# Equal row blocks, interleaved inner tiles and later transposes in the expert stage of a two-layer diffusion transformer

## The chip, the cores and the metric

One core of one Trainium2 chip runs the whole program. The metric is the device time of one execution in microseconds (us), from the first instruction to the end of the program. TensorE (PE) multiplies, ScalarE (ACT) and VectorE (DVE) do the elementwise work, GpSimd (POOL) issues the indirect transfers, SyncE (SP) issues the weight loads.

## The reference, cut to what matters

The model has two layers over 512 image tokens and 256 context tokens, width 1024. Both layers end in a feed-forward part; in the second it is a mixture of 8 experts, of which each token uses 2:

```
gates = sum over the top 2 experts of one_hot * softmax(top logits)
out   = sum over e of gates[:, e] * (silu(x @ w1[e]) * (x @ w3[e])) @ w2[e]
h     = h + g2 * out
```

An expert's inner width is 1408, that is 11 inner tiles of 128. Its first product (w1 and w3) makes the 11 inner tiles, its second product (w2) takes them back to 1024 columns, that is 8 output tiles of 128.

## The kernel before, in words

The kernel computes each expert only for the tokens that chose it. The expert stage runs from about 1290 us to the end. `CAPS` (L33) gives the slots of the eight steps of the stage, in the order in which they run: 176, 192, 96, 176, 112, 152, 136, 128. A step's slots are cut into row blocks of at most 128 (`moe`, L1972): 128 and 48 for 176 slots, 128 and 64 for 192, 24 and 8 remain in the second block of 152 and 136; 96, 112 and 128 are one block.

For each step the rows of its tokens are gathered by an indirect DMA per block (`gather`, L1793), transposed on TensorE and scaled on ScalarE (`prep`, L1821 and L1825, tiles `xtp`, `xaf`, `xT`) while the step before is at its seventh inner tile (`mid`). `expert` (L1832) then works with the tokens in the free dimension:

- First product: for each of 11 inner tiles j, 48 matmuls (8 depth tiles, two matrices, three passes of the split fp16 weights, `mm1` L336) into a PSUM tile `mps` with three buffers (tag "m"). `evac` follows one tile later: ScalarE's silu into `ms` (L1847), VectorE's product into `mgf` (L1848), and after inner tiles 3, 7 and 10 a cast to `mgT` on ScalarE (L1853) and its remainder on VectorE (L1854). The second product reads `mgT`.
- Second product: for each of 8 output tiles d, 33 matmuls (11 inner tiles k, three passes) into `mps2`, of the same tag. `evac2` (L1873) follows one tile later: ScalarE copies PSUM into `my` with the gate (L1876), TensorE transposes `my` block by block into `ytp` (L1880, PSUM tag "t", two buffers), VectorE copies it with the token's weight into `yr` (L1884).
- After the last output tile (`add_rows`, L2009) one indirect accumulating DMA per block adds `yr` to the output in DRAM (L2019). The last step does it in two parts, columns 0 to 639 after d = 4 and the rest after d = 7. Each of these waits for the landing of the one before, as they all write the output.

Weights come as fp32 through `Stream`: SP loads a block (L246), ScalarE casts it to fp16 (`whi`, `whix` or `aT`, L269) and VectorE makes the remainder (`wlo`, `wlox` or `aT`, L274). A load starts when a staging buffer is free again; five blocks are split ahead of the one in use in this stage.

The order in which an engine meets its instructions isn't simply that of the text. The framework plans it: it goes through the instructions with the order of the text as priority, takes for an engine the first one that is ready by its modelled durations, and writes the result out as a fixed order with semaphore waits. A tile whose buffer is still in use waits in this plan until the readers of the older tile are placed. On the chip the engine then keeps this order.

## Time and profile before

| | us |
|---|---|
| median of three runs | 1780.31 |
| lowest and highest | 1778.89 and 1789.47 |
| the profiled execution's own time | 1788.69 |
| its span, first to last instruction | 1786.8 |

The profile is of the one execution in the third line, which lies at the upper end of the runs; all times below are microseconds from the start of its span. PEld are TensorE's weight loads, which overlap its matmuls. The granted clock is the share of 2.4 GHz at which TensorE was let run. A wait names the waiting instruction and the one that released it, in the form out<-in. "L342" is the line of the helper that issues most matmuls, so these are told apart by their tiles: `mps<-xT` is the first product, `mps<-mgT` the second.

### The profile page before, as it was taken

The numbers are of one execution on the slowest core, as the hardware profiler recorded it, in microseconds if no ns is written. First come the engines' busy times: TensorE is split into PE (matmuls) and PEld (weight loads), VectorE is DVE, ScalarE is ACT, GpSimd is POOL, SyncE is SP. The second block draws the span as 40 slices with busy tenths as digits, with TensorE's granted clock in tenths as the row PEclk, the third lists the DMA queues.
The fourth block names the chain that finished last, engine by engine and source line by source line (L and its number), as shares of the span: only waits on it lengthen the run. The fifth ranks groups of instructions, "written<-read, shape, count | busy, mean of one in ns | idle before, by whom it ended". The sixth has DMA issues, their size and how long they took to land. (4 is left out here: it accounts for less than half of the span.)

```text
span 1786.8 us, 36195 instructions
## 1 busy us (share of the span) xinstructions
PE 1668.7 (93%) x15124; PEld 1170.3 (65%) x15124; DVE 1251.0 (70%) x2463; ACT 883.1 (49%) x1420; POOL 156.1 (9%) x102
## 2 busy tenths in 40 slices
PE   3999999999999999999999999989789999999997
PEld 1444666555566665555555466447579988989997
DVE  6784899877665444333147999696898588788884
ACT  6564555262222222111254667564666577677773
POOL 1100000000000000000000000451210113101201
PEclk9999999999999999999999999999799999999999
DMA  8413342534333442233312201101569788899893
GB/s 322 160 51 100 104 166 95 212 117 143 142 129 131 142 142 96 73 112 112 115 61 79 95 1 48 70 3 54 189 204 337 240 312 334 303 330 336 313 337 109
DMA packets 51801, 286.82 MB, mean 161 GB/s; under 512 B 5824, under 2 KB 10944, under 8 KB 27568
## 3 DMA queue, kind: packets, MB, share of 16 engines
q1 hardware_dynamic: 47328, 271.74, 41.8%
q0 software_dynamic: 3296, 10.95, 2.7%
q8 instruction: 120, 1.97, 0.4%
q10 hardware_dynamic: 1008, 1.77, 0.3%
q14 instruction: 49, 0.40, 0.1%
HBM read 272.57 MB, written 11.08 MB: 159 GB/s over the span
## 5 line engine op out<-in xcount | busy, mean ns | idle before, releaser
L342 PEld LDWEIGHTS <-whi 128*128 128x128 f16 x5184 | 469.7, 99 | 185.3 <-issue 10.8
L342 PE MATMUL f<-yT,whi 128*128 128x512 f16 (+1 forms) x1408 | 325.5, 326 | 1.5 <-ACT af L438 1.5
L342 PEld LDWEIGHTS <-wlo 128*128 128x128 f16 x2592 | 255.6, 99 | 90.4 <-issue 2.2
L274 DVE SCALAR_TENSOR_TENSOR wlo<-wst,whi 128x512 f16<-128x512 f32 (+2 forms) x154 | 236.8, 1549 | 68.1 <-ACT whi L269 67.6
L269 ACT ACTIVATE whi<-wst 128x2048 f16<-128x2048 f32 (+2 forms) x152 | 199.4, 1331 | 111.1 <-PE f L342 72.8
L342 PE MATMUL f<-yT,wlo 128*128 128x512 f16 (+1 forms) x704 | 229.1, 326 | 0.0
L375 DVE SCALAR_TENSOR_TENSOR adjk<-wst,srow 128x1024 bf16<-128x1024 f32 x96 | 117.3, 1221 | 98.4 <-DMA wst<-in_w_adr_dram 97.2
L342 PE MATMUL f<-gT,whi 128*128 128x512 f16 (+1 forms) x704 | 164.4, 326 | 0.0
L342 PE MATMUL mps<-xT,whi 128*128 128x176 f16 (+6 forms) x1472 | 149.0, 229 | 3.8 <-DVE mgf L1848 3.7
L342 PE MATMUL mps<-xT,wlo 128*128 128x176 f16 (+6 forms) x736 | 143.0, 229 | 0.0
L342 PE MATMUL f<-gT,wlo 128*128 128x512 f16 (+1 forms) x352 | 114.7, 326 | 0.0
L342 PEld LDWEIGHTS <-aT 128*128 128x128 f16 x1584 | 106.8, 99 | 5.3 <-issue 4.5
L467 DVE TENSOR_TENSOR h<-h,ytp 128x256 f32<-128x256 f32 (+1 forms) x48 | 24.3, 507 | 109.2 <-PE ytp L465 108.9
L2019 POOL DMA_INDIRECT out_dram<-yr,sidx x14 | 54.4, 3885 | 358.3 <-DVE yr L1884 215.3
L342 PE MATMUL cvps<-aT,whi 128*128 128x512 f16 (+1 forms) x384 | 82.6, 328 | 2.8 <-ACT Kl L632 2.3
L342 PEld LDWEIGHTS <-whix 128*128 128x128 f16 x992 | 81.4, 98 | 2.9 <-issue 2.5
L1082 ACT CAST gT<-g 128x512 f16<-128x512 f32 (+1 forms) x23 | 14.0, 608 | 131.0 <-DVE g L1079 131.0
L274 DVE SCALAR_TENSOR_TENSOR wlo<-wstx,whi 128x2048 f16<-128x2048 f32 (+2 forms) x42 | 68.7, 1651 | 14.0 <-ACT whi L269 11.4
L342 PE MATMUL mps<-xT,aT 128*128 128x176 f16 (+6 forms) x1056 | 74.4, 231 | 2.3 <-DVE mgf L1848 2.3
L342 PE MATMUL mps<-mgT,whi 128*128 128x176 f16 (+6 forms) x704 | 73.0, 227 | 0.9 <-ACT mgT L1853 0.9
L342 PE MATMUL mps<-mgT,wlo 128*128 128x176 f16 (+6 forms) x352 | 68.1, 227 | 0.0
L269 ACT ACTIVATE whi<-wstx 128x2048 f16<-128x2048 f32 (+2 forms) x42 | 57.7, 1401 | 17.6 <-PE mps L342 16.3
(398 smaller groups left out, 3490.1 us busy)
## 6 DMA issues: line engine op xcount, KB each, us to landing
wst<-in_w_m_dram SPq DMA_DIRECT2D x38, 1024.0 KB, 6.2
wstx<-in_w_m_dram SPq DMA_DIRECT2D x33, 1024.0 KB, 6.2
wst<-in_w_adr_dram SPq DMA_DIRECT2D x32, 1024.0 KB, 4.9
wst<-in_w_f_dram SPq DMA_DIRECT2D x22, 1024.0 KB, 4.8
wst<-in_w_m_dram SPq DMA_DIRECT2D x27, 704.0 KB, 6.0
wstx<-in_w_m_dram SPq DMA_DIRECT2D x25, 704.0 KB, 6.1
aT<-in_w_m_dram SPq DMA_DIRECT2D x17, 1024.0 KB, 6.2
wst<-in_w_ada_dram SPq DMA_DIRECT2D x12, 1024.0 KB, 4.9
```

Of the source, the lines that this page charges most:

```text
L269: nc.scalar.activation(h, x, AF.Copy, scale=self.scale)
L274: nc.vector.scalar_tensor_tensor(out=l, in0=x, scalar=SW, in1=h, op0=OP.mult, op1=OP.subtract)
L342: mm(ps[:, s0:s0 + sn], w[:, k, :], a[:, kk, s0:s0 + sn], start=first and p == 0, stop=last and p == 2)
L375: nc.vector.scalar_tensor_tensor(out=jk, in0=st[:, j * D:(j + 1) * D], scalar=1.0, in1=self.srow[:, t, :], op0=OP.mult, op1=OP.mult, accum ...
L467: nc.vector.tensor_tensor(out=hs, in0=hs, in1=tp[:, 0:w].rearrange("p (t c) -> p t c", t=nt), op=OP.add)
L1082: nc.any.tensor_copy(gh, g[:, 0:sn])
L2019: self.nc.gpsimd.indirect_dma_start(out=to, out_offset=bass.IndirectOffsetOnAxis(ap=self.sidx[0:sn, e, s:s + 1], axis=0), in_=yr[0:sn, s, ...
```

## The change

It has three parts, all in the expert stage.

- `moe` cuts a step of more than 128 slots into two equal blocks: 88 and 88, 96 and 96, 76 and 76, 68 and 68. Steps of 128 or fewer keep one block. In `route`, the rows to which unused slots are sent are now counted from the same base in both blocks, so that L1765 reads the first column of the table for both.
- In `expert` the second product's matmuls are issued by a new function `part` over a list of inner tiles. For the first two output tiles the text now gives inner tiles 0 to 7 of d = 0, then 0 to 7 of d = 1, then 8 to 10 of d = 0 and 8 to 10 of d = 1. From d = 2 on, the 33 matmuls of a tile follow one another as before.
- `evac2` only makes `my`; the transposes, the copies into `yr` and the call that starts the scatter move to `rows`, which stands at the head of a later iteration. The transposes of a tile d stood behind the matmuls of tile d + 1; they now stand behind those of d + 2. For d = 5, 6 and 7 they all stand behind the matmuls of d = 7. `my` keeps two buffers (`nb` is 2 here).

```diff
--- before.py
+++ after.py
@@ -1762,7 +1762,7 @@
                 x = rp.tile([128, 1], F32, name="free", tag="free", bufs=2)[0:sn]
                 V.tensor_scalar(x, ip[0:sn, s, i, 1:2], -1.0, 1.0, op0=OP.mult, op1=OP.add)
                 y = rp.tile([128, 1], F32, name="to", tag="to", bufs=2)[0:sn]
-                V.tensor_scalar(y, cst[0:sn, tko + i:tko + i + 1], float(NL), None, op0=OP.add)
+                V.tensor_scalar(y, cst[0:sn, tko:tko + 1], float(NL), None, op0=OP.add)
                 V.scalar_tensor_tensor(out=y, in0=y, scalar=x, in1=ip[0:sn, s, i, 0:1], op0=OP.mult, op1=OP.add)
                 if s == NE - 1:
                     V.tensor_scalar(y, y, 8.0, None, op0=OP.mult)
@@ -1872,8 +1872,12 @@
 
         def evac2():
             d, ps = py.pop(0)
-            y = mp.tile([128, cm], F32, name="my", tag="my", bufs=2)[:, 0:C]
+            y = mp.tile([128, cm], F32, name="my", tag="my", bufs=nb)[:, 0:C]
             nc.scalar.activation(y, ps[:, 0, 0:C], AF.Copy, scale=gate[:, d, 0:1])
+            ys.append((d, y))
+
+        def rows():
+            d, y = ys.pop(0)
             tp = pp.tile([128, max(2, len(slots)), 128], F32, name="ytp", tag="t", bufs=2)
             dd = slice(d * 128, (d + 1) * 128)
             for s, (s0, sn) in enumerate(slots):
@@ -1884,15 +1888,35 @@
                     nc.vector.tensor_scalar(yr[0:sn, s, dd], tp[0:sn, s, :], wt[0:sn, s:s + 1], None, op0=OP.mult)
             done(d, yr)
 
+        def part(w, ps, ks):
+            for k in ks:
+                self.mm1(ps[:, 0], *w, k, gT[:, 0], gT[:, 1], seg, k == 0, k == 10)
+
+        ys = []
+        w0 = []
         for d in range(8):
-            wh, wl = (z.rearrange("p (k c) -> p k c", k=11) for z in w2(d))
+            if d > 1 and len(ys) > nb - 1:
+                rows()
+            w = [z.rearrange("p (k c) -> p k c", k=11) for z in w2(d)]
             ps = pp.tile([128, 2, CB], F32, name="mps2", tag="m", bufs=3)
-            for k in range(11):
-                self.mm1(ps[:, 0], wh, wl, k, gT[:, 0], gT[:, 1], seg, k == 0, k == 10)
+            if d < 2 and nb > 1:
+
+                part(w, ps, range(8))
+                w0.append((w, ps))
+                if d == 0:
+                    continue
+                for i in range(2):
+                    part(*w0[i], range(8, 11))
+                    py.append((i, w0[i][1]))
+                evac2()
+                continue
+            part(w, ps, range(11))
             if py:
                 evac2()
             py.append((d, ps))
         evac2()
+        while ys:
+            rows()
 
     def overflow(self):
 
@@ -1969,7 +1993,8 @@
 
     def moe(self, ctx):
         nc, tc = self.nc, self.tc
-        self.slots = [[(0, min(C, 128))] + ([(128, C - 128)] if C > 128 else []) for C in CAPS]
+
+        self.slots = [[(0, C // 2), (C // 2, C // 2)] if C > 128 else [(0, C)] for C in CAPS]
         self.eid = {}
         res = self.A['out'][0:NL].rearrange("(t p) c -> t p c", p=128)
         for t in range(4):
```

## Rows read from the trace of the kernel before

**Rows 1.** The head of the page: the span, then TensorE's busy time, its share of the span and its instructions.

```profile
span 1786.8 us, 36195 instructions
...
PE 1668.7 (93%) x15124; PEld 1170.3 (65%) x15124; DVE 1251.0 (70%) x2463; ACT 883.1 (49%) x1420; POOL 156.1 (9%) x102
```

**Rows 2.** Busy time by stretch, in the expert stage, two answers one under the other: the stretch, its length, then busy us and (x instructions) of PE, PEld, DVE, ACT, POOL, and at the end the granted TensorE clock (1.00 is 2.4 GHz, 0.50 is 1.2 GHz), the DMA share and GB/s.

```profile
1350.00:1450.00 100.00, 98.18 (x1167) 93.83 (x1165) 71.65 (x76) 61.58 (x71) 6.62 (x3) 1.00 0.81 290
1500.00:1750.00 250.00, 241.98 (x3653) 231.05 (x3651) 212.83 (x223) 182.78 (x219) 42.70 (x11) 1.00 0.92 328
...
1470.00:1475.00 5.00, 5.00 (x34) 3.42 (x34) 2.35 (x4) 2.51 (x6) 0.00 (x0) 0.50 1.04 359
1475.00:1480.00 5.00, 5.00 (x64) 4.91 (x65) 3.06 (x4) 3.10 (x6) 2.49 (x2) 0.51 0.72 254
1480.00:1485.00 5.00, 5.00 (x121) 5.00 (x118) 3.42 (x4) 3.94 (x5) 0.00 (x0) 1.00 0.70 224
```

**Rows 3.** Who TensorE waited for between 1330 us and the end: waiting line, releaser, us in total, how often, the longest.

```profile
PE mps L342 <- DVE mgf L1848: 6.6, 7, 3.7
PE ytp L1880 <- ACT my L1876: 5.4, 12, 1.1
PE mps L342 <- ACT mgT L1853: 1.9, 5, 0.5
PE ytp L1880 <- DVE yr L1884: 1.9, 8, 0.4
```

**Rows 4.** Who the queue of weight loads (SP) waited for between 1340 us and the end, the longest of the list; L246 is the line that issues a weight load.

```profile
SPq L246 <- DVE yr L1884: 142.2, 48, 6.5
SPq L246 <- DVE mgf L1848: 129.2, 51, 5.1
```

**Rows 5.** TensorE in order of time at the start of the second product of the first expert (176 slots): start, length, the merged instructions, their number, and in brackets the idle time before and its releaser.

```profile
1355.24 3.73 PE L342 MATMUL mps<-mgT,aT 128*128 128x176 f16 x47
1359.38 0.39 PE L342 MATMUL mps<-mgT,aT 128*128 128x176 f16 x3 [0.41 <-ACT mgT L1853]
...
1363.11 0.33 PE L1880 MATMUL ytp<-ident,my 128*128 128x128 f32 x1 [0.25 <-ACT my L1876]
...
1364.04 0.27 PE L1880 MATMUL ytp<-ident,my 128*128 128x128 f32 x1
```

**Rows 6.** The same for the fourth expert (176 slots).

```profile
1542.28 1.98 PE L342 MATMUL mps<-mgT,aT 128*128 128x176 f16 x24
1544.10 0.32 PE L342 MATMUL mps<-mgT,whi 128*128 128x176 f16 x2
...
1544.56 0.32 PE L342 MATMUL mps<-mgT,whi 128*128 128x176 f16 x2
1545.28 0.24 PE L342 MATMUL mps<-mgT,aT 128*128 128x176 f16 x1 [0.41 <-ACT mgT L1853]
```

**Rows 7.** ScalarE, then VectorE, over the same moment as group 5, in order of time.

```profile
1355.37 1.38 ACT L269 ACTIVATE whix<-wstx 128x1408 f16<-128x1408 f32 x1 [2.06 <-PE mps L342]
...
1358.69 0.64 ACT L1853 ACTIVATE mgT<-mgf 128x528 f16<-128x528 f32 x1 [1.74 <-DVE mgf L1848]
...
1356.78 1.63 DVE L274 SCALAR_TENSOR_TENSOR wlox<-wstx,whix 128x1408 f16<-128x1408 f32 x1 [1.76 <-ACT whix L269]
```

**Rows 8.** The third expert (96 slots), in order of time: TensorE's longest wait for a transpose, then ScalarE.

```profile
1491.01 0.32 PE L1880 MATMUL ytp<-ident,my 128*96 128x128 f32 x1 [1.12 <-ACT my L1876]
...
1488.81 1.91 ACT L269 ACTIVATE whix<-wstx 128x2048 f16<-128x2048 f32 x1 [1.04 <-PE mps L342]
1490.63 0.56 ACT L1876 ACTIVATE my<-mps,gate 128x96 f32<-128x96 f32 x2
...
1492.88 0.57 ACT L1876 ACTIVATE my<-mps,gate 128x96 f32<-128x96 f32 x2
```

**Rows 9.** Groups by form: the transposes of TensorE, of the gathered rows (xtp, weights of the block's rows, the block's columns streamed) and of the second product (ytp, weights of the block's columns, 128 streamed): line, engine, operation, forms, count, busy us and mean ns of one, idle us before and its releasers.

```profile
L1880 PE MATMUL ytp<-ident,my 128*128 128x128 f32 x48 | 14.1, 294 | 3.4 <-ACT my L1876 1.8 <-DVE yr L1884 0.9
...
L1821 PE MATMUL xtp<-ident,xg 128*128 128x128 f32 x40 | 12.6, 320 | 2.2 <-ACT xaf L1825 1.8
...
L1880 PE MATMUL ytp<-ident,my 128*48 128x128 f32 x16 | 4.5, 286 | 0.5 <-DVE yr L1884 0.3
...
L1821 PE MATMUL xtp<-ident,xg 48*128 48x48 f32 x8 | 2.6, 319 | 0.0
...
L1821 PE MATMUL xtp<-ident,xg 96*128 96x96 f32 x8 | 2.1, 280 | 0.2
...
L1821 PE MATMUL xtp<-ident,xg 8*128 8x8 f32 x8 | 1.8, 223 | 0.0
```

**Rows 10.** The end, in order of time: TensorE, VectorE and GpSimd at the last expert's transposes and its two scatters; the last row is of the chain that ended last, the landing of the first scatter.

```profile
1770.93 0.28 PE L1880 MATMUL ytp<-ident,my 128*128 128x128 f32 x1
...
1772.89 0.28 PE L1880 MATMUL ytp<-ident,my 128*128 128x128 f32 x1
...
1775.89 0.35 DVE L1884 TENSOR_SCALAR yr<-ytp,ws 128x128 f32<-128x128 f32 x1 [0.38 <-PE ytp L1880]
...
1771.88 1.59 POOL L2019 DMA_INDIRECT out_dram<-yr,sidx  x1 [27.11 <-DVE yr L1884]
1778.05 1.56 POOL L2019 DMA_INDIRECT out_dram<-yr,sidx  x1 [4.58 <-DMA out_dram<-yr,sidx]
...
1771.88 5.41 DMA out_dram<-yr,sidx
```

## The prediction

> **What bounds the kernel now.** I read the head of the page first, then busy time by stretch, then TensorE's waits, then the waits of the load queue, and last the moments at which the change acts. TensorE is busy 93% of the span [rows 1], and in the expert stage more: 98.18 of 100 us in the first two experts and 241.98 of 250 us from 1500 to 1750, at a granted clock of 1.00 [rows 2]. VectorE and ScalarE stand at 212.83 and 182.78 of the same 250 us, so both have room; DMA stands at 0.92. Is it the loads that bound the stage? The load queue says no: its longest waits, 142.2 and 129.2 us, are for VectorE, behind whose instructions a staging buffer comes free [rows 4]. Loads start when TensorE and the engines that split weights make room, and in the list of TensorE's waits no weight appears [rows 3]. So the stage goes at TensorE's pace, and time saved on TensorE's queue is saved at the end, as long as the splits follow.
>
> What is there to save? From 1330 us on TensorE waits 5.4 us for `my` before transposes (12 times), 1.9 us for `yr`, 1.9 us for the cast `mgT`, and 6.6 us for `mgf`, of which one wait alone is 3.7 us [rows 3]; that one is in a first product, which the change doesn't touch. What the change aims at is then 5.4 + 1.9 + (6.6 − 3.7) = 10.2 us, 0.6% of the span, and it can't remove more than that by itself.
>
> **The change, part by part.**
>
> Interleaved inner tiles. The text now asks for 24 matmuls of d = 0, 24 of d = 1, and then inner tiles 8 to 10, which need the last cast. But the order on TensorE is planned, and the trace shows that the plan already does this: in the first expert 47 recorded matmuls of the second product run before the first one that waits for `mgT`, not 24 [rows 5]. The text of before would give 24 (8 inner tiles by 3 passes). So for this expert nothing changes, and the wait of 0.41 us stays: it comes from ScalarE's 1.38 us split and VectorE's 1.63 us split, which run while the last silu and product are due, so that the cast starts only at 1358.69 [rows 7]. No more cover is to be had either, as `mps` has three buffers and the last inner tile still holds one. In the fourth expert the plan put fewer in front: 24, then 8 of the next tile, up to 1544.9, and then 0.41 us of waiting [rows 6]. Sixteen more matmuls at (1544.10 − 1542.28) / 24 = 0.076 us are 1.2 us, more than that wait: it goes. The waits of this kind sum to at most 1.9 + 2.9 = 4.8 us [rows 3] over eight experts; if three experts are like the fourth, with 0.35 us each, about 1 us goes. Bounds: 0 (the plan draws the same order again) and 4.8 us. I take 1, nearer to the first expert's row, since the cover is the same 48 there.
>
> Transposes one tile later. 104 transposes stay 104; their copies and scatters stay too, only their place moves. The trace shows them already some way into the next tile's matmuls (1363.11 and 1364.04 with ten between, and the first still waited 0.25 us for `my`) [rows 5]. One tile later `my` has another 33 matmuls of time, 2.5 us at the pace of 0.076 us worked out above. The waits for `my` were at most 1.1 us each [rows 3], so nearly all of the 5.4 us should go. Not where ScalarE itself is behind: in the third expert it makes two `my` in 0.56 us, then splits for 1.91 us, then makes two again, at 1490.63 and 1492.88 [rows 8], 2.25 us apart, so that there ScalarE's splits set the pace; the longest wait, 1.12 us, moves rather than goes. I leave 1.1 us standing and take 5.4 − 1.1 = 4.3 us. Bounds: 5.4, and 0 if the later place only meets the next instruction that is late. What is queued behind such a transpose? All of TensorE's matmuls. What does `my` wait for? With two buffers, ScalarE's copy of tile d + 2 now waits for the transposes of d; those stand at the very point where the matmuls of d + 2 are done, so ScalarE loses about the length of two transposes, and the splits behind it are covered by its idle 67 of 250 us [rows 2]. The waits for `yr` (1.9 us) come from the second transpose of a tile and its two PSUM buffers; these stay, and I count 0 for them.
>
> Equal blocks. `ytp` takes as long for 48 columns as for 128 (286 and 294 ns), so two blocks cost two transposes, before and after: 0. `xtp` does depend on its columns: 128 and 48 cost 320 + 319 ns, and two of 88 by the row for 96 cost 2 x 280 = 560; 128 and 8 cost 320 + 223 = 543, and two of 68 by the same row 560 [rows 9]. Over eight depth tiles that is −0.6 us for one step and +0.1 us for another. With four steps affected the sum is between −2 and +1 us; these durations overlap with neighbours and partly lie in a slow-clock stretch, so I take 0. VectorE, ScalarE and GpSimd issue as many instructions as before; the gathers and scatters keep their number, and only the rows in each are shared out evenly. They are hidden, except for the last expert's, and that one has 128 slots, one block, and stays as it is.
>
> The end. Here the change costs. The last step's first scatter starts after d = 4. Its transpose is at 1770.93, the next one at 1772.89: one tile is 1.96 us. The second scatter has its rows ready at 1775.89 + 0.35 = 1776.24, but it starts at 1778.05, since it waits for the first one's landing, 5.41 us after 1771.88 [rows 10]. So the end hangs on the transpose of d = 4, which moves one tile back: +1.96 us, and the slack is nil. Bounds: +1.96, and +0.2 if the plan pulls that transpose forward to where it stood. The matmuls of d = 6 have priority in the text and are ready all the time, so I take +2.0. The three transposes that now follow the last matmul (d = 5, 6, 7, 0.3 us each) end before that scatter lands and cost nothing.
>
> The clock. At 1470 to 1480, after transposes with a wait among them, the granted clock is 0.50 and 0.51, the 1.2 GHz level, and TensorE runs 64 matmuls in 5 us where the next 5 us hold 121 at 1.00 [rows 2]. Through the transposes of the second products, which have matmuls between them, it stays at 1.00 (1350 to 1450) [rows 2]. The Trainium skill (TensorE: Matmul & The Clock Gate, Part 4: PE-mode transpose) says that a transpose doesn't count as work for the clock as a matmul does. By that rule, six transposes drawn together behind d = 7 could lose the clock; the rows agree for the stretch at 1470 and give no case of it in a second product. In the sum I put 0 for it, as the plan has the next expert's matmuls to put between, and it is a rival below.
>
> **Sum.** −1.0 − 4.3 + 0 + 2.0 = −3.3 us. The profiled execution took 1788.69 us, so it would take 1785.4. It lies 8.4 us above the median of the runs shown; the stalls named here don't depend on which run is taken, so I put the same −3.3 on the median: 1780.31 − 3.3 = 1777.0 us.
>
> **The rivals.**
>
> A. The change does not do what it says. The planned order is already interleaved [rows 5], and the deferred transposes may be put where the plan thinks best and wait there again. Then only the later first scatter is left: 1780.3 + 2.0 = 1782. For it speak the 47 matmuls, against it that the transposes' new place in the text is behind a whole tile.
>
> B. Slower through the clock. The transposes of d = 5, 6 and 7 meet the copies of VectorE (`ytp` has two buffers) at an expert's end, TensorE stands still between them, and the clock falls as at 1470. One such fall, 5 us of clock from 10 us at half [rows 2], costs 5 us, and with a wait before it as long as the longest before a transpose today, 1.1 us [rows 3], 6 us: 1783. In all five steps of two blocks it makes 1777 + 5 x 6 = 1807. It decides the sign from the first fall on, since 6 is more than the 3.3 of the sum. Against it: the next expert's matmuls are ready and have been placed between such transposes before.
>
> C. A larger gain. The plan is drawn anew from the first changed instruction on, so a stall that costs the clock today may vanish: whatever leads to the stretch at 1.2 GHz, with its 5 us [rows 2], or the one wait of 3.7 us for `mgf` [rows 3]. With the first gone the time is 1777 − 5 = 1772, with both 1777 − 8.7 = 1768. Nothing in the diff aims at them.
>
> **How the numbers follow.** My forecast, between 1772 and 1780 by its bounds: 0.50. A: 0.22. B: 0.13, of which 0.04 for four or five experts. C: 0.15. The predicted time is the forecast's 1777. The range takes in A, the forecast, C with both stalls and B with one fall and the spread of the runs: 1766 to 1787; left out are B with more falls and a larger redrawing, together under 0.2. A measurement of this kernel can tell about 1% from no change, that is 17.8 us. Below 1762.5 only several lost stalls together would lead: 0.05. Above 1798.1 only B in four or five experts: 0.04. Within 1%: 0.91.
>
> **What the profile of the changed kernel would show.** The wait of `ytp` for `my` should fall from 5.4 us to about 1; if it stays above 4, rival A holds. The waits for `mgT` should shrink by no more than a fifth or so, and 48 matmuls should stand before the first of them in every expert. `xtp` and `ytp` should keep their sums. The transpose of d = 4 of the last expert should be one tile, 1.96 us, nearer to the end, and the time from it to the end of the span should be as before, 1786.8 − 1770.9 = 15.9 us; if the first scatter starts as early as before, that step of mine is wrong. Granted clocks should stay at 1.00 from 1350 on but for the stretch around 1470; a stretch at 0.5 around an expert's end means B. I would be wrong as a whole if the loads, or the splits on VectorE, began to make TensorE wait: then weights would appear among its releasers.

## The result, and the profile after

The changed kernel takes 1798.99 us, the median of eight runs (1793.81 to 1802.17). The kernel before, run beside it, takes 1785.14 us (eight runs). The ratio is 1.0075 with a 95% interval of 1.0061 to 1.0089, so the change costs 0.0075 x 1785.1 = 13.4 us. I had forecast a gain of 3.3 us, and the time lies outside my range. The profiled execution took 1801.01 us.

First the head of the page after, then its lines on transfers, under them the same two lines of the page of before. The columns of a queue are packets, MB, and the share of 16 DMA engines.

```profile
span 1799.2 us, 36176 instructions
PE 1659.2 (92%) x15124; PEld 1167.5 (65%) x15124; DVE 1250.8 (70%) x2463; ACT 883.1 (49%) x1420; POOL 144.1 (8%) x102
DMA packets 53737, 286.83 MB, mean 159 GB/s; under 512 B 7760, under 2 KB 12880, under 8 KB 29504
q0 software_dynamic: 5232, 10.96, 2.8%
```

```profile
DMA packets 51801, 286.82 MB, mean 161 GB/s; under 512 B 5824, under 2 KB 10944, under 8 KB 27568
q0 software_dynamic: 3296, 10.95, 2.7%
```

TensorE does the same number of matmuls as in [rows 1]. What differs is GpSimd's queue q0, which carries the gathers and scatters: 5232 packets in place of 3296, with nearly the same bytes (10.96 and 10.95 MB). All 1936 new packets are under 512 bytes (7760 − 5824 = 1936). The span's loss is in few places, which TensorE's waits from 1330 us to the end show (waiting line, releaser, us in total, times, longest); they answer to [rows 3].

```profile
PE ytp L1884 <- DVE yr L1888: 14.2, 11, 11.2
PE mps L342 <- DVE mgf L1848: 13.5, 9, 5.5
PE ytp L1884 <- ACT my L1876: 6.9, 9, 1.5
PE mps L342 <- DVE mgT L1854: 0.7, 2, 0.4
PE mps L342 <- ACT mgT L1853: 0.5, 2, 0.3
```

The wait for `yr` grew from 1.9 to 14.2 us, and 11.2 of that is one wait. The wait for `my`, which was to fall to about 1 us, rose from 5.4 to 6.9. (Of the 13.5 us for `mgf`, 5.5 lie at 1339 us, ahead of the first second product, where before has 3.7.) Where is the one wait of 11.2 us? In order of time: TensorE, VectorE and GpSimd around 1710 us, the start of the seventh step's transposes.

```profile
1707.70 0.27 PE L1884 MATMUL ytp<-ident,my 128*68 128x128 f32 x1
1720.51 0.43 PE L1884 MATMUL ytp<-ident,my 128*68 128x128 f32 x1 [11.17 <-DVE yr L1888]
...
1720.10 0.35 DVE L1888 TENSOR_SCALAR yr<-ytp,ws 68x128 f32<-68x128 f32 x1 [10.51 <-DMA out_dram<-yr,sidx]
...
1674.80 12.78 POOL L2044 DMA_INDIRECT out_dram<-yr,sidx  x1 [58.30 <-DVE mgf L1848]
1703.81 1.82 POOL L2044 DMA_INDIRECT out_dram<-yr,sidx  x1 [16.22 <-DVE mgf L1848]
```

Read it from the end. TensorE's second transpose needs its PSUM buffer back from VectorE's copy into `yr`. That copy waits for a transfer out of `yr`: there is one `yr`, and the sixth step's scatters still read it. Its second scatter is issued at 1703.81 and lands at 1720. It starts so late because it waits for the first to land, and GpSimd needed 12.78 us to issue that first one. (The row of 1703.81 names VectorE as its releaser; the same wait in the experiment e6_gather16 below, 15.07 us, is put down to `out_dram<-yr,sidx`, the landing, and VectorE's `yr` was done long before.) From 1710 to 1720 nearly everything stands still (ScalarE works for 1.4 us), as busy time by stretch shows. It is the last line here; the others answer to [rows 2] (stretch, length, busy us and instructions of PE, PEld, DVE, ACT, POOL, granted clock, DMA share, GB/s).

```profile
1350.00:1450.00 100.00, 97.44 (x1160) 93.36 (x1158) 71.21 (x75) 61.95 (x70) 6.20 (x3) 1.00 0.81 291
1500.00:1750.00 250.00, 231.39 (x3532) 223.44 (x3530) 204.62 (x215) 177.12 (x212) 32.00 (x10) 0.98 0.89 316
1470.00:1475.00 5.00, 5.00 (x109) 4.86 (x109) 3.60 (x7) 4.89 (x9) 2.67 (x2) 1.00 1.02 422
1475.00:1480.00 5.00, 4.27 (x102) 4.16 (x99) 5.00 (x7) 3.75 (x6) 0.00 (x0) 1.00 0.99 268
1710.00:1720.00 10.00, 0.00 (x0) 0.00 (x0) 0.00 (x0) 1.40 (x1) 0.00 (x0) 0.70 0.51 158
```

The stretch of half clock at 1470 is gone: the clock is 1.00 there, and 109 and 102 matmuls run where 34 and 64 did. So the changed kernel was ahead before 1700 us: the seventh step's second product starts at 1701.0 us, before at 1708.1. It then lost more than that: from there to the last step's second product it takes 67.2 us, before 50.1. In these 17.1 us are the stall, the half clock that follows it (0.79 on average from 1720 to 1730) and a wait of 4.3 us for `mgf` in the last step, 0.6 there before. ScalarE, then TensorE:

```profile
1755.53 1.38 ACT L269 ACTIVATE whix<-wst 128x1408 f16<-128x1408 f32 x1 [6.92 <-DMA wst<-in_w_m_dram]
...
1758.82 0.37 PE L342 MATMUL mps<-xT,whi 128*128 128x128 f16 x2 [4.33 <-DVE mgf L1848]
```

ScalarE's cast waits 6.92 us for a weight load. The silu behind it, and so VectorE's `mgf`, comes late by that. The order of the work came out as predicted in two places, at the start of the first expert's second product (answers to [rows 5]) and at the end (to [rows 10]).

```profile
1355.07 3.80 PE L342 MATMUL mps<-mgT,aT 128*128 128x176 f16 x48
1359.21 0.31 PE L342 MATMUL mps<-mgT,aT 128*128 128x176 f16 x2 [0.34 <-ACT mgT L1853]
...
1782.96 0.28 PE L1884 MATMUL ytp<-ident,my 128*128 128x128 f32 x1
...
1783.91 1.58 POOL L2044 DMA_INDIRECT out_dram<-yr,sidx  x1 [26.00 <-DVE yr L1888]
1789.94 1.56 POOL L2044 DMA_INDIRECT out_dram<-yr,sidx  x1 [4.46 <-DMA out_dram<-yr,sidx]
```

### The profile page after: what moved, and what is told of

It reads as the page before. It is cut to its first block, busy times and chain, and to the rows that moved or that the text cites. A ratio compares the mean times of both kernels' runs of the same rounds, so it can differ in the third digit from the quotient of the medians.

```text
span 1799.2 us, 36176 instructions
## 1 busy us (share of the span) xinstructions
PE 1659.2 (92%) x15124; PEld 1167.5 (65%) x15124; DVE 1250.8 (70%) x2463; ACT 883.1 (49%) x1420; POOL 144.1 (8%) x102
## 2 busy tenths in 40 slices
DMA packets 53737, 286.83 MB, mean 159 GB/s; under 512 B 7760, under 2 KB 12880, under 8 KB 29504
## 3 DMA queue, kind: packets, MB, share of 16 engines
q0 software_dynamic: 5232, 10.96, 2.8%
## 5 line engine op out<-in xcount | busy, mean ns | idle before, releaser
L274 DVE SCALAR_TENSOR_TENSOR wlo<-wst,whi 128x512 f16<-128x512 f32 (+2 forms) x154 | 236.7, 1548 | 69.5 <-ACT whi L269 69.1
L269 ACT ACTIVATE whi<-wst 128x2048 f16<-128x2048 f32 (+2 forms) x152 | 199.3, 1330 | 112.4 <-PE f L342 71.7
L274 DVE SCALAR_TENSOR_TENSOR wlo<-wstx,whi 128x2048 f16<-128x2048 f32 (+2 forms) x42 | 68.8, 1651 | 14.6 <-ACT whi L269 14.6
L2044 POOL DMA_INDIRECT out_dram<-yr,sidx x14 | 41.7, 2979 | 372.0 <-DVE yr L1888 192.5
```

The costliest lines, as they stand in the source:

```text
L269: nc.scalar.activation(h, x, AF.Copy, scale=self.scale)
L274: nc.vector.scalar_tensor_tensor(out=l, in0=x, scalar=SW, in1=h, op0=OP.mult, op1=OP.subtract)
L2044: self.nc.gpsimd.indirect_dma_start(out=to, out_offset=bass.IndirectOffsetOnAxis(ap=self.sidx[0:sn, e, s:s + 1], axis=0), in_=yr[0:sn, s, ...
```

## The experiments

All were compared with the kernel before on the same chip, whose median was 1786 to 1788 us in each set. Each ratio below is to it, with its 95% interval.

**Which part costs?** Four kernels ran together. At first two theories stood: R, that the new row counts make gathers and scatters dearer, and O, that the new order on TensorE does the harm.

The first is before with only the new blocks (and the base of L1765 that goes with them):

```diff
-        self.slots = [[(0, min(C, 128))] + ([(128, C - 128)] if C > 128 else []) for C in CAPS]
+        self.slots = [[(0, C // 2), (C // 2, C // 2)] if C > 128 else [(0, C)] for C in CAPS]
```

> The kernel before with the equal blocks alone (the order of the second product and the transposes as before). Theory R (row counts): a gather or scatter whose rows are no multiple of 16 is moved with hundreds of extra packets of 4 or 8 bytes and lands after 10 to 17 us in place of 2 to 8; VectorE's first copy into yr of the seventh step waits for such a scatter, and weight loads land late beside it. It expects most of the loss here: 8 to 16 us slower than the kernel before, 76 x 3 = 228 and 68 x 3 = 204 extra packets per scatter of the sixth and seventh step, and a wait of TensorE of several us at the start of the seventh step's second product. Theory O (order): the loss comes from the transposes that stand one tile later, so that scatters start later. It expects the time of before within 3 us.

Measured: 1792.72 us, 1.0033 (1.0017 to 1.0049), about +6 us. No wait for the scatter's landing is in its trace (the longest for `yr` is 0.4 us). Theory R had expected that wait and 8 to 16 us in this kernel, and missed both.

The second is after with the old blocks, that is the same two lines the other way round; interleave and later transposes stay.

> The changed kernel with the blocks of before (128 and the rest): only the interleaved inner tiles and the later transposes are left. Theory R expects no long wait for yr and, by my own sum, between 5 us faster and 3 us slower than the kernel before: the waits for my shrink, the last expert's first scatter starts 1.96 us later. Theory O expects the loss here, 8 to 16 us slower than before, with the wait for yr of 11 us in it.

Measured: 1786.17 us, 0.9996 (0.9982 to 1.0011). The order alone neither costs nor gains.

The third is after with blocks whose size is rounded up to a multiple of 16 rows: 96 and 96, 80 and 80. The two blocks overlap, and the doubled slots have weight 0 in the second.

```diff
-        self.slots = [[(0, C // 2), (C // 2, C // 2)] if C > 128 else [(0, C)] for C in CAPS]
+        self.slots = [[(0, -(-C // 32) * 16), (C - -(-C // 32) * 16, -(-C // 32) * 16)] if C > 128 else [(0, C)] for C in CAPS]
...
+                if i and s0 < sn:
+                    V.memset(self.ws[0:sn - s0, s, 1:2], 0.0)
```

> The changed kernel with its two equal blocks rounded up to a multiple of 16 rows each: 96 and 96 for 176 and 192 slots, 80 and 80 for 152 and 136; the second block begins earlier, so that some slots stand in both, and their weight in the second is set to zero. It moves up to 24 more rows per step than the changed kernel. Theory R expects that the packets of 4 and 8 bytes go but for the 16 or so of each transfer, that each scatter lands within 8 us or so of its start, that no wait for yr is over 1 us, and that the time is at or below the kernel before: between 8 us faster and 2 us slower. Theory O expects the time of the changed kernel, 12 to 16 us slower than before.

Measured: 1784.36 us, 0.9988 (0.9973 to 1.0003). The whole loss is gone, though the blocks are still equal, more rows are moved, and the order is that of after. TensorE's longest wait for `yr` is 0.6 us, and its page has this line for q0:

```profile
q0 software_dynamic: 3376, 11.41, 2.9%
```

The fourth is after with the `yr` of the last two steps in the two buffers of `xg`, which are free by then, so that no row copy waits for a scatter.

```diff
-        yr = mp.tile([128, max(2, len(slots)), D], F32, name="yr", tag="yr", bufs=1)
+        yp, yt, yb = (self.xgp, "xg", 2) if yrx else (mp, "yr", 1)
+        yr = yp.tile([128, max(2, len(slots)), D], F32, name="yr", tag=yt, bufs=yb)
```

> The changed kernel, with the copies of the last two steps (yr) in the buffers of the gathered rows, which are free by then, so that they need not wait for the scatters of the step before; the slow scatters stay. If the loss is the wait for yr alone, this gives back about 11 us: within 4 us of the kernel before. If the weight loads that land late beside the slow transfers carry it as well, only part comes back: 4 to 8 us slower than before, with the wait of 4.3 us at the inner tiles of the last step still there. Theory O expects no more than 3 us back.

Measured: 1793.33 us, 1.0036 (1.002 to 1.0052). The long wait is gone, and with it 0.0039 of the ratio, 7 us; what is left is as much as equal blocks cost alone. Theory R holds and O falls. But the parts don't add up: +6 for the blocks and 0 for the order make 6 of 13.4. The other 7 to 8 us belong to both together, and need a theory of their own.

**Is it the row count, and whose?** Two kernels, run together with the next two. The first halves only the steps of 152 and 136 slots and keeps 128 + 48 and 128 + 64:

```diff
-        self.slots = [[(0, C // 2), (C // 2, C // 2)] if C > 128 else [(0, C)] for C in CAPS]
+        self.slots = [[(0, C // 2), (C // 2, C // 2)] if 128 < C < 176 else [(0, min(C, 128))] + ([(128, C - 128)] if C > 128 else []) for C in CAPS]
```

> The kernel after, but only the steps of 152 and 136 slots are halved (76+76, 68+68); those of 176 and 192 keep 128+48 and 128+64 as before. Theory R (what costs is a row count that is not a multiple of 16 in gathers and scatters): the four tables of 76 and 68 rows carry the packets, so q0 keeps nearly all of its extra packets over before (3296 before, 5232 after; expected about 4900 to 5100), the wait of some 11 us for the sixth step's second scatter ahead of the seventh step's first row copy stays, and the time is 1794 to 1799. Theory E (equal blocks cost by being equal: two middle-sized tables per step instead of a large and a small one, whatever the numbers): half of the steps are undone, so about half of the loss goes, 1789 to 1793, and the wait falls under 6 us.

Measured: 1797.62 us, 1.0067 (1.0044 to 1.009); q0 has 4992 packets, and the wait is 10.2 us. Tables of 76 and 68 rows carry all of the loss that can be told from that of after. The second rounds every gather up to a multiple of 16 rows and leaves the scatters:

```diff
+        nc.gpsimd.memset(self.idx, 0)
...
+            sn = -(-sn // 16) * 16
```

> The kernel after with every gather rounded up to a multiple of 16 rows (the index buffer is set to zero first, so that the added rows read row 0 and are not used); scatters keep 76 and 68 rows. Theory S (scatters alone make the stall: one row buffer waits for their landing): the gathers of the sixth step shrink from 16.7 us of packets to under 8, the wait of some 11 us stays within 2 us, the time is 1794 to 1799. Theory G (gathers share the queue with the scatters and push them back): the scatters of the sixth step land 5 us or more earlier, the wait falls to 6 us or less, the time is 1786 to 1791.

Measured: 1797.9 us, 1.0066 (1.0043 to 1.0088), the wait 11.0 us, as theory S expected. So the stall is the scatters' doing. What the gathers cost, this total can't tell, since its interval reaches 4 us to either side; the traces tell it, as the next section shows.

The packets of q0 themselves, from all fourteen traces, by the table they belong to. A row is one packet of 4 KB. The small packets hold 4 or 8 bytes and come on top of 16 of 4 bytes that every transfer has. The times are of scatters of whole rows whose packets can be told from a neighbour's.

```
rows in the table    small packets   first to last packet, us              row packets in flight at once, at most
128, 112, 96, 80     none            3.3-6.6, 4.1-5.1, 2.7-6.1, 2.3-5.4    15-22
88                   40              3.8-7.9                               11-17
76                   228 (3 a row)   8.3-13.3                              5-7
68                   204 (3 a row)   7.2-11.4                              5-7
24, 8                8               2.6-3.3, 1.7-2.2                      7-11, 4-6
```

The row packets themselves take as long in each of these scatters (0.33 to 0.50 us on average). What differs is how many are under way together. Theory R's words were too broad: 88, 24 and 8 rows are no multiple of 16 either, and their scatters stay short.

These counts give the new packets exactly. After has six tables of 88 rows (four scattered, two gathered; the first step's rows are not gathered this way), four of 76 and four of 68, and no longer the four tables of 24 and 8: 6 x 40 + 4 x 228 + 4 x 204 − 4 x 8 = 1936.

**Do the later transposes save anything by themselves?** Before with later transposes only, old blocks, no interleave (in the text of after, two conditions):

```diff
-            if d < 2 and nb > 1:
+            if d < 2 and nb > 9:
...
-        self.slots = [[(0, C // 2), (C // 2, C // 2)] if C > 128 else [(0, C)] for C in CAPS]
+        self.slots = [[(0, min(C, 128))] + ([(128, C - 128)] if C > 128 else []) for C in CAPS]
```

> The kernel before with the later transposes alone (own gate-product buffer per tile, rows one tile later), without the interleave and with the old blocks. My prediction gave this step -4.3 us: TensorE's waits of transposes for the gate product 5.4 us to about 1.1 between 1330 us and the end, plus about 2 us at the end. Theory P (the step does this, and other parts spoil it): waits for the gate product under 2.5 us, time 1782 to 1784. Theory O (the gate product is late for another reason than the distance, so the distance moves nothing): waits for the gate product still 4 to 7 us, time 1785 to 1789.

Measured: 1786.64 us, 0.9999 (0.9983 to 1.0015), waits for `my` 6.1 us, as theory O expected. The step by itself is worth nothing. One row of its trace is of use for the interaction, the issue of the sixth step's first scatter, with 128 rows; under it the same scatter before:

```profile
1669.15 12.58 POOL L2044 DMA_INDIRECT out_dram<-yr,sidx  x1 [59.67 <-DVE mgf L1848]
```

```profile
1679.42 1.58 POOL L2019 DMA_INDIRECT out_dram<-yr,sidx  x1 [56.42 <-DVE yr L1884]
...
1678.55 0.59 DVE L1884 TENSOR_SCALAR yr<-ytp,ws 128x128 f32<-128x128 f32 x2
1679.83 0.30 DVE L1848 SCALAR_TENSOR_TENSOR mgf<-mps,ms 128x136 f32<-128x136 f32 x1 [0.69 <-ACT ms L1847]
```

So a long issue doesn't need a row count like 76. Before, the scatter met 0.69 us in which VectorE did nothing. In e7_late_only it starts at 1669.15, just after VectorE has begun a weight remainder (L274, 2.27 us, at 1669.01), and VectorE has no gap until 1680.5. In after it is the same:

```profile
1674.62 2.28 DVE L274 SCALAR_TENSOR_TENSOR wlox<-wstx,whix 128x2048 f16<-128x2048 f32 x1
1676.82 0.34 DVE L1888 TENSOR_SCALAR yr<-ytp,ws 76x128 f32<-76x128 f32 x1
...
1685.81 0.29 DVE L1848 SCALAR_TENSOR_TENSOR mgf<-mps,ms 128x136 f32<-128x136 f32 x1
1686.42 1.62 DVE L274 SCALAR_TENSOR_TENSOR wlo<-wstx,whi 128x1408 f16<-128x1408 f32 x1 [0.32 <-ACT whi L269]
```

The scatter starts at 1674.80, VectorE's first gap is at 1686.1, the issue ends at 1687.6.

**Does VectorE hold up the issue?** A theory from rows alone, so it was given its own test: after with one pause for VectorE behind the first scatter of the sixth step. GpSimd copies one word behind the issue, and VectorE waits for that word.

```diff
+            if e == 5 and s == 0:
+                g = self.ms.tile([1, 2], F32, name="gap", tag="gap", bufs=1)
+                self.nc.gpsimd.tensor_copy(g[:, 0:1], yr[0:1, 0, D - 1:D])
+                self.nc.vector.tensor_copy(g[:, 1:2], g[:, 0:1])
```

> The kernel after with one pause for VectorE: right behind the last row copies of the sixth step it copies one word that GpSimd copies behind the issue of that step's first scatter, so VectorE must stand still until the scatter is issued. In after that issue took 12.78 us (from 1674.80), with VectorE busy from 1655 to 1686. Theory L (GpSimd cannot finish the issue while VectorE is busy): the issue falls to 2 to 5 us, the second scatter of the step is issued 8 to 11 us earlier, the 11.2 us wait of the seventh step's first transposes for a row copy falls under 3 us, and the time is 1786 to 1793 although VectorE loses 2 to 4 us. Theory N (the issue is long for its 76 rows or for the queue): it stays over 10 us, VectorE stands still for as long, and the time is 1799 or more.

Measured: 1791.32 us, 1.0027 (1.0012 to 1.0042). GpSimd, then VectorE, in its trace in order of time:

```profile
1678.70 3.79 POOL L2044 DMA_INDIRECT out_dram<-yr,sidx  x1 [58.41 <-DVE mgf L1848]
1681.81 0.73 POOL L2049 COPY gap<-yr 1x1 f32<-1x1 f32 x1
1693.63 1.83 POOL L2044 DMA_INDIRECT out_dram<-yr,sidx  x1 [11.10 <-DVE mgf L1848]
...
1682.57 0.14 DVE L2050 COPY gap<-gap 1x1 f32<-1x1 f32 x1 [1.51 <-POOL gap L2049]
```

A pause of 1.51 us shortens the issue from 12.78 to 3.79 us, the second scatter goes out 15 us after the first one's start and not 29, and the wait of 11.2 us is gone (the longest for `yr` is 0.6 us): 0.0075 − 0.0027 = 0.0048, 8.6 us. Of the 14 us by which the second scatter comes sooner, 9 are the issue; the other 5 are the first scatter's packets, which take 8.3 us here and 13.0 in after. So VectorE's work does hold up this issue.

Theory L's words, that GpSimd cannot finish an issue while VectorE is busy, go too far, though. In after the fifth step's scatter starts just as the sixth's, within a remainder, and VectorE has no gap from 1610.4 to 1620 (VectorE, GpSimd, VectorE):

```profile
1612.85 2.28 DVE L274 SCALAR_TENSOR_TENSOR wlo<-wst,whi 128x2048 f16<-128x2048 f32 x1
1613.21 3.30 POOL L2044 DMA_INDIRECT out_dram<-yr,sidx  x1 [26.80 <-DVE yr L1888]
1615.05 0.30 DVE L1848 SCALAR_TENSOR_TENSOR mgf<-mps,ms 128x152 f32<-128x152 f32 x1
```

The issue ends 1.4 us behind the end of that remainder. The sixth step's ends 1.7 us behind the end of one too (1685.89), but only after it let five such instructions end before. Which end lets GpSimd through, no run shows.

**Which order part brings the long issue?** Equal blocks with later transposes but no interleave (the first condition of e7_late_only), and equal blocks with the interleave but transposes as before:

```diff
-            if d > 1 and len(ys) > nb - 1:
+            if d > 1 and len(ys) > 0:
```

> The change without the interleave: equal blocks and later transposes. Equal blocks alone gave 1.0033, the order parts alone 0.9996, the whole change 1.0075. Theory I (the later transposes move the sixth step's first scatter out of VectorE's gap, and together with long scatters this makes the stall): issue of that scatter over 10 us, the wait for the landing 8 to 12 us, ratio 1.006 to 1.008. Theory J (it is the interleave that does so): issue of 1.6 to 3 us, no wait over 2 us there, ratio 1.002 to 1.004.

> The change without the later transposes: equal blocks and the interleave, transposes where they were before. Theory I: the first scatter of the sixth step is issued in VectorE's gap in 1.6 to 3 us, no wait over 2 us for its landing, ratio 1.002 to 1.004. Theory J: issue over 10 us, wait 8 to 12 us, ratio 1.006 to 1.008.

Measured: 1800.14 us, 1.0081 (1.0061 to 1.0101), with 12.78 us of issue and a wait of 12.2 us; and 1791.47 us, 1.0017 (1.0002 to 1.0031), with 1.83 us of issue and no wait over 0.4 us. Theory I holds in both, though the wait of 12.2 us and both ratios lie a little outside its numbers. GpSimd's first scatter of the sixth step, in e10_blocks_late and under it in e11_blocks_interleave:

```profile
1678.17 12.78 POOL L2044 DMA_INDIRECT out_dram<-yr,sidx  x1 [58.39 <-DVE mgf L1848]
```

```profile
1681.30 1.83 POOL L2044 DMA_INDIRECT out_dram<-yr,sidx  x1 [55.30 <-DVE yr L1888]
```

**A version without the loss.** e3_round16, with the last step's transposes where they stood before:

```diff
-            if d > 1 and len(ys) > nb - 1:
+            if d > 1 and len(ys) > (nb - 1 if late else 0):
...
-                                xT, mp, pp, lambda d, yr: self.add_rows(e, d, yr), self.ws[:, e, :], mid)
+                                xT, mp, pp, lambda d, yr: self.add_rows(e, d, yr), self.ws[:, e, :], mid, late=e < NE - 1)
```

> Blocks rounded up to multiples of 16 rows (96+96, 80+80 overlapping, the doubled slots with weight 0 in one of the two), interleave and later transposes, but in the last step each tile's transposes stand where they stood before. Theory T (the later transposes lengthen the end by about 2 us and nothing else there matters): last matmul to the end 12 us instead of 14.3, time about 1782, that is 2 us under e3_round16 (1784.4) and 4 under before. Theory 0 (the end is set by something else): within 1 us of e3_round16.

Measured: 1783.05 us, 0.9985 (0.9967 to 1.0003). From the last matmul to the end of the span it is 13.1 us, not 12 (14.2 in e3_round16). The time is 1.3 us below e3_round16, and the intervals of the two overlap: undecided.

Last, the same with ScalarE's copy moved ahead of the request for the next weights in the text:

```diff
+            if d > 1 and py:
+                evac2()
             w = [z.rearrange("p (k c) -> p k c", k=11) for z in w2(d)]
...
             part(w, ps, range(11))
-            if py:
-                evac2()
```

> e8_best with ScalarE's copy of a second-product tile (my) put ahead of the casts of the weights that the next tile asks for, instead of behind them. Theory C (the transposes wait because the copy stands behind a 1.9 us cast on ScalarE, not because they stand too near): waits for the gate product fall from 5.8 us to under 3 us, and the time goes to 1780 to 1783. Theory D (the casts then come late themselves): those waits fall, but waits for weights grow by as much, and the time is 1783 to 1787.

Measured: 1782.35 us, 0.9975 (0.9961 to 0.9989), the only kernel here that is faster than before by more than its interval. But the waits for `my` are 6.8 us, not under 3, so theory C isn't borne out. It wasn't put to a real test either, since on ScalarE the copies still stand behind a cast, as in the third expert:

```profile
1481.26 1.91 ACT L269 ACTIVATE whix<-wstx 128x2048 f16<-128x2048 f32 x1 [1.04 <-PE mps L342]
1483.08 0.56 ACT L1878 ACTIVATE my<-mps,gate 128x96 f32<-128x96 f32 x2
```

Against e8_best (0.9967 to 1.0003) the gain is within the intervals.

## Why the prediction was wrong

**Equal blocks: 0 counted, +6 us measured, and half of a stall.** This is the step that failed: "the gathers and scatters keep their number, and only the rows in each are shared out evenly. They are hidden, except for the last expert's". Their number is kept, but they don't stay hidden. With 76 or 68 rows a scatter's packets stretch over 7.2 to 13.3 us, and rounding up to 80 rows takes that away together with the loss (e3_round16); rounding the gathers alone leaves the stall (e6_gather16). I priced the instructions (`xtp`, `ytp`, issues) and not the transfers, although tables of 128, 112, 96, 64, 48, 24 and 8 rows were all that the trace had, so that the price of 76 rows was one that it didn't show. I should have bounded it from both sides and kept the upper end in the range.

How the +6 us come about without the stall, the traces show by where the time is lost. The first two lines are the stretch from the third step's second product to the fourth's, before and in e1_blocks (columns as in [rows 2]), the other two TensorE's wait for `my` in it, before and in e1_blocks.

```profile
1483.93:1542.28 58.35, 54.91 (x812) 53.31 (x810) 46.98 (x46) 41.87 (x51) 19.56 (x3) 1.00 0.93 331
1479.09:1542.50 63.41, 55.27 (x813) 53.37 (x811) 47.74 (x46) 42.47 (x51) 7.67 (x3) 1.00 0.94 317
...
PE ytp L1880 <- ACT my L1876: 2.2, 4, 1.1
...
PE ytp L1880 <- ACT my L1876: 6.9, 6, 2.9
```

Here e1_blocks loses 5.1 us, and no scatter of 76 or 68 rows is near. What runs here is the gather of the sixth step's two tables of 76 rows. In six traces (after, e1_blocks, e4_yr_free, e9_gap, e10_blocks_late, e11_blocks_interleave) its last packet comes 20 to 23 us after its first issue, and the stretch takes 59.9 to 63.9 us; in the other eight it comes after 5 to 12 us, and the stretch takes 58.3 to 58.9 us. The eight have old or rounded tables there, but for e5_odd_only, whose gather of 76 and 76 rows was done after 9.7 us. From the seventh step's second product to the eighth's, where the scatters run, e1_blocks loses another 2.2 us. So in this trace most of the loss is the gathers'.

What such a transfer holds up is weight loads. Between 1370 and 1750 us of the fourteen traces, a load with no transfer of GpSimd beside it lands 5.7 us after its issue (median of 255), beside a scatter of 80 to 128 rows (88 left out) after 7.2 us (106), of 76 or 68 rows after 9.5 us (35), and beside a gather of 76 and 76 rows after 11.5 us (15). ScalarE's casts wait for loads for 13.9 us in all from 1330 us on before, 24.4 us in e1_blocks, 12.6 in e2_order and 13.8 in e3_round16. All of these transfers use the same 16 DMA engines, but no run tells how one slows the other. My sign for this, weights among TensorE's releasers, was a bad one: there are none after, and the late loads show in the waits for `mgf` and `my`, which ScalarE makes late behind such a cast.

**The interaction: nothing counted, 7 to 9 us measured.** The chain has two links, and each alone is harmless. Later transposes move the sixth step's first scatter from a gap of VectorE to the start of a remainder (e10_blocks_late has it, e11_blocks_interleave hasn't), and its issue takes 12.6 us in place of 1.6 (e7_late_only, e2_order 12.57); with old or rounded blocks it lands soon enough, and nobody waits. Row counts of 76 make two scatters of that step, one behind the other, several us longer; issued at once they land in time (e1_blocks, e11_blocks_interleave). Together they end past the point at which the seventh step needs `yr`, of which there is one. In the prediction I asked what is queued behind a transpose and what waits for `my`, and not what waits for the scatter that moves with it. "GpSimd issue as many instructions as before" counted issues, not their lengths, and [rows 10] showed only issues of 1.6 us. The trace of before had long ones elsewhere, and I hadn't read them, as here behind the third step's rows:

```profile
1504.21 17.63 POOL L2019 DMA_INDIRECT out_dram<-yr,sidx  x1 [25.93 <-DVE yr L1884]
```

**Later transposes: −4.3 us forecast, about 0 measured** (0.9999 alone). The waits for `my` went from 5.4 to 6.1 us, not to 1.1. Where they are has changed. By stretch of one step, before had 2.2 us in the third step, 1.3 in the fifth and at most 0.9 in any other; after has 3.7 and 2.6 in these two, 0.2 in the sixth, 0.4 in the last and none elsewhere; e7_late_only, with the old tables, has 1.1, 2.9 and 0.2 in the third, fifth and sixth, 1.4 in the seventh and 0.5 in the last. So one tile more distance does what I said in most of the steps with many slots, and there was little to save there. In the third and fifth step, of 96 and 112 slots, ScalarE sets the pace. ScalarE in the third expert after, in order of time, answers to [rows 8]:

```profile
1484.50 0.55 ACT L1876 ACTIVATE my<-mps,gate 128x96 f32<-128x96 f32 x2
1486.79 1.91 ACT L269 ACTIVATE whix<-wstx 128x2048 f16<-128x2048 f32 x1 [1.74 <-DMA wstx<-in_w_m_dram]
1488.61 0.55 ACT L1876 ACTIVATE my<-mps,gate 128x96 f32<-128x96 f32 x2
```

The copies stand behind a cast, and the cast waits 1.74 us for its load. From 1475 to 1480 the DMA share is 0.99. A later transpose can't make up for a load that is late; I had seen this in [rows 8] and left 1.1 us for it, which is one wait of it and not the sum of two steps. That the loads set the pace in these two steps is read from the rows; no run took them away.

**What was right.** The interleave was in the plan already: in the first expert 48 matmuls stand before the first wait for `mgT` where 47 were recorded, and these waits went from 1.9 to 0.5 + 0.7 = 1.2 us, where I had forecast that they fall by 1.0; without the interleave they are 1.9 us (e7_late_only, e10_blocks_late). The end: from the last matmul to the end of the span it is 14.3 us, before 12.0, so +2.3 where I had +2.0. Equal blocks as such cost TensorE nothing: e3_round16, which has them, is as fast as e2_order with the old ones. Rival B was not seen: the granted clock is 1.00 from 1350 to 1710 us, across six experts' ends, and falls with the long stall (0.70 from 1710 to 1720) and behind the late load (0.50 from 1758.5 to 1761.5). Rival C happened by half, the half clock at 1470 us is gone. It is gone in e1_blocks and e2_order too (1.00 there from 1470 to 1480), so no part of the change owns it, and e2_order with it is still no faster than before. Rival A had the right mechanism for the transposes, waits above 4 us, and no price for the blocks.

My sum, by what was measured: interleave and later transposes, with the end in them, 0 (e2_order, 0.9996) in place of −3.3; blocks +6 in place of 0; and the two together 7 to 8 more. The 22.0 us between my 1777.0 and the measured 1798.99 hold 4.8 us of the base besides: the three runs that I had of before gave 1780.31, the eight beside the change 1785.14.

## What to carry to other kernels

An indirect transfer is priced by its row count, and 76 rows were a new price, not the old one in other shares: here rounding up to a multiple of 16 took it away, even at the cost of moving rows twice. A late load need not show as a wait for weights; look also at what the engine that casts them makes next. Where a transfer reads a tile that has a single buffer, write down when it is issued, how long the issue takes, when it lands and when the buffer's next writer comes; two changes that each use up a part of that slack can be free alone and dear together. More distance between two instructions helps against latency and not where an engine or the loads set the pace, so add up a wait by steps before taking it off.

## What the runs showed of the hardware that I had not expected

**Rows in multiples of 16.** Scatters of 128, 112, 96 and 80 rows take 2.3 to 6.6 us, those of 76 and 68 rows 7.2 to 13.3 us, with three packets of 8 bytes added for each row. The Trainium skill ("DMA: Bandwidth & Descriptors", section "Why a DMA increments its semaphore by 16 and not by 1") says that a transfer is spread over the largest number of engines up to 16 that divides the slowest dimension of both sides. By that rule 76 and 68 rows would go over 4 engines and 80 over 16; 19 rows for an engine against 5 is an estimate of 3.8 times the time by that page, and the medians are 11.2 us for 76 rows and 3.5 us for 80, that is 3.2 times. For 88 rows it would be 11 engines of 8 rows each, an estimate of 1.6 times, and the median is 5.0 us. The trace's packets don't say which engine carried them, but two counts agree with that rule: at most 5 to 7 row packets are in flight with 76 and 68 rows and 15 to 22 with 80 to 128 (88 left out), and the small packets are as many as if each of the 16 engines that has no rows got one for every row of one that has: 12 x 19 = 228, 12 x 17 = 204, 5 x 8 = 40 for 88 rows, 4 x 2 = 8 for 24 and 8 x 1 = 8 for 8. This rule spoke against the change, and I hadn't weighed it.

**VectorE can hold up the issue of a scatter.** The sixth step's first scatter took 12.4 to 12.8 us in all ten kernels with later transposes and no pause, whatever its row count, 1.6 to 1.8 us in before, e1_blocks and e11_blocks_interleave, 3.79 us with a pause of 1.51 us put in. The Trainium skill ("SBUF — State Buffer", section "Who interferes with whom") says that VectorE and GpSimd share a pair of ports, that a VectorE instruction with two operands in SBUF contends for it with a GpSimd instruction that reads SBUF, and that the one which comes first keeps it. The remainders of L274 are such instructions, and the traces agree so far: all 20 issues over 4 us in the fourteen traces end 1.3 to 1.7 us behind the end of such an instruction. They differ from the same section in one thing: it reports that a `tensor_tensor`, also with two operands, did not stall transfers that GpSimd issues. And by the rows it is more than one instruction's wait: in after VectorE ran ten instructions from the scatter's start to the end of the one that let it through, six of them with two operands in SBUF. A gap of VectorE isn't what ends the wait: the issue of 17.63 us above ended at 1521.84, and VectorE's first gap began at 1522.32.
